# Output products of six heads as seven block products instead of eight, with block sums on GpSimd

## The chip, the cores and the metric

The kernel runs on one core of a Trainium2 chip. The metric is the device time of one execution in microseconds; the profile is one further execution, recorded by the hardware profiler. Engines are named as in the profile: PE is TensorE, DVE is VectorE, ACT is ScalarE, POOL is GpSimd, SP is SyncE, whose queue issues nearly all DMAs.

## What is computed

An encoder trunk of two layers, applied to two independent groups of 512 tokens with 1024 features: one layer of differential attention, one of bidirectional retention. Both end alike, and only that end is touched by the change: a head's 256-wide mixer output is normalised per token, multiplied by a gate, and all eight heads go through one output projection that is added to the residual.

```python
def diff_attention(h, w_in, lq1, lk1, lq2, lk2, subln_g, w_out, lambda_init):
    ...
    o = rms_norm(o, subln_g, SUBLN_EPS) * (1.0 - lambda_init)
    o = o.reshape(B, S, D_INNER) * jax.nn.silu(gate)
    return o @ w_out

def bidir_retention(h, w_in, decay_fwd, decay_bwd, subln_g, w_out):
    ...
    o = rms_norm(o_f + o_b, subln_g, SUBLN_EPS)
    o = o.reshape(B, S, D_INNER) * jax.nn.silu(gate)
    return o @ w_out
```

For one head, one half of a group's tokens and all 1024 output features, the projection is a product of a 256x256 block (tokens by head features) with a 256x1024 block of weights.

## The kernel before

Every fp32 operand of a matmul is split into a high part (cast by ACT, `hi_of`, L481) and a low part (the rest, subtracted by DVE, `lo_of`, L484), and a product is three matmuls (`PASSES`): high by high, high by low, low by high. PE runs, in order: the input projections of layer 1 (to about 610 us; already in seven-product form), the attention heads (to about 1015 us), the input projections of layer 2 (to about 1480 us), the retention blocks, one per head and group (to the end).

In the attention stage a loop runs over 64 tiles (head, group, 128 query tokens): scores (L1546), row maximum on DVE (L1554), exponentials on ACT, a factor from DVE's reciprocal (L1573) and POOL (L1574), a combining add on DVE (L1576), transposes (L1587), and per pair of tiles the product with v (L1607). In the retention stage a block has scores, two states and two chunks of outputs (L1864, L1872; on DVE L1879 and L1883). In both, `weigh` then gates the output (`og`, L1191), splits it into `oT`, and squares it; the two halves of the squares are added on DVE (L1196). `norm_cols` or `weighed_both` turn the squares into `rr`, one factor per token, with a reciprocal root on POOL (L1211, L1912).

`owe` then puts four output steps on the list `todo`, for two token tiles and two column halves of 512. `out_step` issues, for each, six matmuls (two blocks of 128 features by three passes, L1279) into a fresh `pj` bank of PSUM, and one scaled add on DVE (L1284) that multiplies by `rr` and adds to the residual in SBUF. `out_weights` loads 256x512 of weights when they are first needed and splits them with one instruction of 1024 columns each on ACT and DVE. `fill` takes steps from `todo` between other work; `settle` empties a head's steps before the next head reuses its `oT`. There are three `pj` banks; in attention every second transpose takes one too.

None of this is issued at once. Each call records an operation with its engine, an assumed duration and its readers and writers (`Plan.op`); `Plan.arrange` then lists them with a planner: PE takes operations in program order, at most 24 places ahead of the first that isn't done, the others by a due time. `Plan.issue` repeats this with random shifts of due times from the table `SHIFTS` (a time, how far back, how large, what share, a seed). The result is a fixed order for each engine.

Of the kernel before, what the change touches and what calls it, by code (L numbers as in the profile page):

```python
# [10 lines left out]
F32 = mybir.dt.float32  # L11
# [25 lines left out]
LAG = 4  # L37

# [11 lines left out]
class Buf:  # L50
# [237 lines left out]
def trunk_kernel(  # L288
# [22 lines left out]
    places = {}  # L311
    cnt = [0]

    def view(pool, tag, i, size, shape, dt=F32):


        n = math.prod(shape[1:])
        if (tag, i) not in places:
            if size <= 32 and pool in (cp, wk):
                k = next(k for k, used in enumerate(gaps) if used + size <= (1024 + PAD - RING if k < WS_BUFS - 1 else 56))  # L320
                places[tag, i] = pads[k][:, gaps[k]:gaps[k] + size]
                gaps[k] += size
            else:
                places[tag, i] = pool.tile([P, size], F32, tag=f"{tag}{i}", name=f"{tag}_{i}", bufs=1)
        t = places[tag, i][0:shape[0], 0:n]
        if dt != F32:
# [74 lines left out]
    def raw_t(shape, bufs=4):  # L401

        n = math.prod(shape[1:])

        def make(i):
            t = view(wk, "raw", i, n, [P, n]) if i < 4 else both_ring(F32)[:, 0:n]
# [9 lines left out]
    def c_t(name="c"):  # L416
        return work("c", [P, S], 4, name=name)

    def e_t(name="e"):
        return work("e", [P, S], E_BUFS, name=name)  # L420

    def m_t(name="m"):
        return work("m", [P, S], 4, name=name)
# [761 lines left out]
    def weigh(y, sg, oT, c, scale=1.0, sq=None):  # L1185
# [3 lines left out]
        og, sq = c_t("og"), sq or m_t("sq")  # L1189
# [6 lines left out]
        dve(256, lambda: nc.vector.tensor_tensor(sq[:, 0:256], sq[:, 0:256], sq[:, 256:512], op=ALU.add), [sq], [sq])  # L1196
# [93 lines left out]
    def owe(w, h, g, t, o, rr, last):  # L1290
        for i in range(2):
            owed[h, g] = owed.get((h, g), 0) + 1
            parts = 2 if w is wo2 and (h, g, t, i) == (NH - 1, NG - 1, NT - 1, 1) else 1
            todo.append(lambda i=i, parts=parts: out_step(w, h, g, t, i, o, rr, last, parts))

# [300 lines left out]
    def av(i):  # L1596
# [17 lines left out]
        st[i].update(o=o, sq=weigh(o, sg[h, g], oT[h, g], t // 2, GUARD))  # L1614

    def weighed(i):
# [72 lines left out]
    for i in range(FIRST, N + 4, 2):  # L1689
# [13 lines left out]
        fetch_next(i)  # L1703
    while todo:
        fill(1)
# [23 lines left out]
    Fs, aTs, sqs = {}, {}, {}  # L1729
# [13 lines left out]
    def decay(h):  # L1743
# [4 lines left out]
        mid = m_t("mid")  # L1748
        mid2 = m_t("mid")
# [104 lines left out]
    def av2(b, c):  # L1854
# [32 lines left out]
        sqs[b, c] = weigh(y, sg[b], oT[h, g], c, sq=st_t([P, S], "sq"))  # L1887
# [8 lines left out]
    def weighed_both(b):  # L1896
# [7 lines left out]
        for c in range(2):  # L1904
# [7 lines left out]
            pool(200, lambda ss=ss, rr=rr: nc.gpsimd.tensor_tensor(rr.t, ss.t, mhalf[:, 0:2], op=ALU.pow), [ss, mhalf], [rr])  # L1912
            for n in range(2):
# [173 lines left out]
```

## Time and profile before

| | |
|---|---|
| median of 3 runs | 1782.05 us (1781.91 to 1782.11) |
| the profiled execution | 1782.33 us, of which the span is 1780.2 us |
| instructions | 28,644 |
| output products (L1279) | 1,542 matmuls |
| scaled adds (L1284) | 257 |

In the page's first part each engine has its busy time, its share of the span and its instructions. Groups are named by line, engine, operation, and output<-inputs; "busy, mean ns | idle before, releaser" stand behind. A timeline row is a start, a duration, and the instruction, with a wait in brackets. Busy times include the tail of an instruction in which the next may already have begun.

### The profile page before, as it was taken

The numbers are of one execution on the slowest core, as the hardware profiler recorded it, in microseconds if no ns is written. First come the engines' busy times: TensorE is split into PE (matmuls) and PEld (weight loads), VectorE is DVE, ScalarE is ACT, GpSimd is POOL, SyncE is SP. The second block draws the span as 40 slices with busy tenths as digits, with TensorE's granted clock in tenths as the row PEclk, the third lists the DMA queues.
The fourth block names the chain that finished last, engine by engine and source line by source line (L and its number), as shares of the span: only waits on it lengthen the run. The fifth ranks groups of instructions, "written<-read, shape, count | busy, mean of one in ns | idle before, by whom it ended". The sixth has DMA issues, their size and how long they took to land.

```text
span 1780.2 us, 28644 instructions
## 1 busy us (share of the span) xinstructions
PE 1769.7 (99%) x10485; PEld 1565.0 (88%) x10485; DVE 1550.6 (87%) x2660; ACT 926.9 (52%) x1947; POOL 118.5 (7%) x256
## 2 busy tenths in 40 slices
PE   9999999999999999999999999999999999999998
PEld 7889988888998888888888888899889988988887
DVE  8979779999979888888888898887998797888887
ACT  8664434544544565455455876444544455444446
POOL 1000000000000011111111100000000001111114
PEclk9999999999999999999999999999999999999999
DMA  6345535555555695455453624464565579665562
GB/s 233 102 153 168 177 118 160 171 160 168 190 175 155 218 332 187 174 189 190 168 190 105 213 77 155 138 200 166 172 206 179 176 222 407 236 232 194 217 221 95
DMA packets 162819, 328.85 MB, mean 185 GB/s; under 512 B 12772, under 2 KB 76920, under 8 KB 162680
## 3 DMA queue, kind: packets, MB, share of 16 engines
q1 hardware_dynamic: 162352, 326.71, 54.6%
q8 instruction: 82, 1.34, 0.3%
q14 instruction: 57, 0.47, 0.1%
q10 hardware_dynamic: 328, 0.34, 0.1%
HBM read 209.55 MB, written 117.44 MB: 184 GB/s over the span
## 4 chain that ended last, share of the span: by engine, by line
PE 98%; ACT 1%; DMA 1%; DVE 0%; issue 0%; POOL 0%; SPq 0%; POOLq 0%; DVEq 0%; ACTq 0%
PE pj L756 21%; PE pj L1279 19%; PE sc L756 11%; PE pj L766 10%; PE o L756 6%; PE o L1607 5%; PE sc L1546 5%; PE sc L766 5%; PE o L905 3%; PE o L991 2%; PE o L1864 1%; PE tp L1843 1%; PE sc L1816 1%; PE sc L1864 1%; PE pj L1587 1%; PE tp L1587 1%
## 5 line engine op out<-in xcount | busy, mean ns | idle before, releaser
L1279 PE MATMUL pj<-ws,arena 128*128 128x512 f32 (+1 forms) x1334 | 344.8, 390 | 0.0
L1279 PEld LDWEIGHTS pj<-ws,arena 128*128 128x128 f32 x1334 | 247.7, 188 | 50.4
L756 PE MATMUL pj<-b,ws 128*128 128x512 f32 x1080 | 263.5, 390 | 0.0
L481 ACT CAST ws<-st 128x512 fp32r<-128x512 f32 x264 | 161.1, 622 | 162.3 <-PE sc L756 37.5
L756 PEld LDWEIGHTS pj<-b,ws 128*128 128x128 f32 x1080 | 200.0, 188 | 40.4 <-issue 0.3
L484 DVE TENSOR_TENSOR ws<-st,ws 128x512 fp32r<-128x512 f32 x264 | 178.3, 687 | 50.8 <-ACT ws L481 38.4
L1284 DVE SCALAR_TENSOR_TENSOR b<-pj,pad,b 128x512 f32<-128x512 f32 (+1 forms) x257 | 189.6, 745 | 29.8 <-PE pj L1279 16.9
L756 PE MATMUL sc<-arena,ws 128*128 128x512 f32 x768 | 186.0, 390 | 0.0
L756 PEld LDWEIGHTS sc<-arena,ws 128*128 128x128 f32 x768 | 142.7, 188 | 28.9
L756 PE MATMUL pj<-arena,ws 128*128 128x512 f32 x636 | 156.0, 390 | 0.0
L756 PEld LDWEIGHTS pj<-arena,ws 128*128 128x128 f32 x636 | 118.8, 188 | 24.6 <-DVE ws L484 0.2
L481 ACT CAST ws<-raw 128x512 fp32r<-128x512 f32 (+2 forms) x140 | 103.2, 741 | 63.4 <-PE o L905 15.5
L484 DVE TENSOR_TENSOR ws<-raw,ws 128x512 fp32r<-128x512 f32 (+2 forms) x135 | 109.2, 813 | 23.4 <-ACT ws L481 21.1
L1564 ACT ACTIVATE b<-sc,pad 128x512 f32<-128x512 f32 x128 | 87.5, 691 | 74.3 <-DVE pad L1554 74.1
L766 PE MATMUL pj<-ws,b 128*128 128x256 f32 x960 | 116.1, 275 | 0.0
L766 PEld LDWEIGHTS pj<-ws,b 128*128 128x128 f32 x960 | 112.5, 188 | 0.3
L756 PE MATMUL o<-arena,ws 128*128 128x512 f32 x456 | 108.3, 390 | 0.4 <-DVE b L544 0.4
L1546 PE MATMUL sc<-arena 128*128 128x512 f32 x384 | 101.8, 398 | 0.7 <-ACT b L1564 0.7
L809 ACT COPY c<-pj 128x512 f32<-128x512 f32 x96 | 56.3, 588 | 87.1 <-PE pj L756 64.2
L756 PEld LDWEIGHTS o<-arena,ws 128*128 128x128 f32 x456 | 85.3, 188 | 18.3 <-DVE b L544 0.6
L481 ACT CAST os<-e 128x512 fp32r<-128x512 f32 x88 | 54.8, 622 | 77.6 <-DVE e L817 29.2
L1607 PEld LDWEIGHTS o<-arena 128*128 128x128 f32 x768 | 93.0, 188 | 2.4
(307 smaller groups left out, 3233.8 us busy)
## 6 DMA issues: line engine op xcount, KB each, us to landing
qk<-os SPq DMA_DIRECT2D x192, 256.0 KB, 3.6
arena<-qk SPq DMA_DIRECT2D x96, 512.0 KB, 7.0
v<-os SPq DMA_DIRECT2D x64, 512.0 KB, 3.6
arena<-v SPq DMA_DIRECT2D x64, 512.0 KB, 4.1
raw<-in_da_w_in_dram SPq DMA_DIRECT2D x51, 512.0 KB, 5.6
raw<-in_ret_w_in_dram SPq DMA_DIRECT2D x38, 512.0 KB, 5.0
os<-g SPq DMA_DIRECT2D x32, 512.0 KB, 7.2
g<-e SPq DMA_DIRECT2D x48, 256.0 KB, 4.2
```

What stands on the lines that cost most here:

```text
L481: act(n, lambda: nc.scalar.copy(dst(), src()), r, w)
L484: dve(n, lambda: nc.vector.tensor_tensor(dst(), src(), hi().bitcast(F32), op=ALU.subtract), r, w)
L756: nc.tensor.matmul(ps.t, a[u][0]()[:, k, :], bt[k][:, v, :], start=(opens and k == 0 and i == 0), stop=(k == 3 and i == 2), skip_group_che ...
L766: nc.tensor.matmul(ps[:, (t % 2) * 256:(t % 2) * 256 + 256], bt[k][:, v, t * P:(t + 1) * P], a[u][0]()[:, k, :], start=(opens and t % 2 == ...
L809: act(S, lambda c=c, ps=ps: nc.scalar.copy(c.t, ps.t), [ps], [c])
L905: nc.tensor.matmul(ps[:, c0:c0 + 256], w[:, lo:lo + P], of(b, j), start=(start and j == 0 and i == 0), stop=(j == 1 and i == 2), skip_grou ...
L991: nc.tensor.matmul(ps[:, t * 256:t * 256 + 256], of(b, j, t), w[:, a, j], start=(start and t == 0 and j == 0 and i == 0), stop=(j == 1 and ...
L1279: nc.tensor.matmul(ps[:, here], o[a][:, e, t * P:(t + 1) * P], u[b][:, e, here], start=(m == 0), stop=(m == 5))
L1284: axpy(n, lambda half=half, here=here, ps=ps: nc.vector.scalar_tensor_tensor(half, ps[:, here], rr[:, t % 2:t % 2 + 1], half, op0=ALU.mult ...
L1546: nc.tensor.matmul(s.t, q[:, a, t * P:(t + 1) * P], k[:, b, :], start=(n == 0), stop=(n == 2))
L1564: act(840, lambda j=j, s=s, m=m: nc.scalar.activation(p[:, j, :], s.t, AF.Exp, bias=m.t, accum_out=sm[:, 2 * j + n:2 * j + n + 1]), [s, m] ...
L1607: nc.tensor.matmul(o[:, e * 256:(e + 1) * 256], v[b][:, j, e * P:(e + 1) * P], aT[a][:, j, :], start=(n == 0), stop=(n % 12 == 11), skip_g ...
```

## The change

In heads 2, 4 and 6 of the attention layer and 1, 3 and 5 of the retention layer, the output product of a head and a token half is split in two by two by two: tokens in two tiles of 128, features in two blocks of 128, columns in two halves of 512. Its eight block products become seven, P1 to P7. They need sums of blocks of the weights (T1 to T4, once per head, in `fast_weights`) and of the gated output (s1 to s4, for each group and token half, in `block_sums`). The sums are computed on POOL, then split by ACT and DVE; the addition of the squares of these heads moves to POOL as well. Three `pj` banks x, y and z collect the products: x takes P1, P6, P7 and P4 one upon the other, z takes P5 and P3, y takes P2. Each product is followed by a scaled add into one of the four output blocks, so there are seven adds where there were four.

```diff
+FAST = (2, 4, 6,), (1, 3, 5,)
...
-    (635.39, 16, 2, 0.05, 454008), (1473.67, 30, 2, 0.2, 912168), (1473.67, 8, 2, 0.2, 596270),
+    (13.25, 30, 1, 1, 761111), (1599.01, 16, 4, 0.2, 176783), (636.31, 30, 0.3, 0.5, 131788),
...
+    def either(on, n, out, a, b, op, r, w):
+        plan.op(on, 0.2+0.0036*n if on == "POOL" else 0.07 + 0.00104 * n, lambda: (
+            nc.gpsimd if on == "POOL" else nc.vector).tensor_tensor(out(), a(), b(), op=op), r, w)
+
+    def block_sums(og, new):
+        x, hi, lo = st_t([P, S], "sums"), *(n(dt=F32R) for n in new)
...
+        for k, (o, a, b, fn, r) in enumerate((
+                (s1, a21, a22, ALU.add, [og]), (s2, s1, a11, ALU.subtract, [og, (x, 0)]),
+                (s3, a11, a21, ALU.subtract, [og]), (s4, a12, s2, ALU.subtract, [og, (x, 1)]))):
+            either('POOL', P, o, a, b, fn, r, [(x, k)])
+        hi_of(S, lambda: hi.t, lambda: x.t, [x], [hi])
+        lo_of(S, lambda: lo.t, lambda: x.t, lambda: hi.t, [x, hi], [lo])
+        return hi, lo
...
-        dve(256, lambda: nc.vector.tensor_tensor(sq[:, 0:256], sq[:, 0:256], sq[:, 256:512], op=ALU.add), [sq], [sq])
+        if sums is not None:
+            sums.append(block_sums(og, new))
+        either("POOL" if sums is not None else "DVE", 256, lambda: sq[:, 0:256], lambda: sq[:, 0:256],
+               lambda: sq[:, 256:512], ALU.add, [sq], [sq])
...
+    def fast_weights(w, h, t12):
+        r = [raw_t([P, 2, S]) for _ in range(2)]
...
+        hi_of(1024, lambda: hi.t, lambda: r[0].t, [r[0]], [hi])
+        lo_of(1024, lambda: lo.t, lambda: r[0].t, lambda: hi.t, [r[0], hi], [lo])
...
+        either('POOL', S, lambda: x[0].t, b12, b11, ALU.subtract, r, [x[0]])
+        parts("t1", t12[0](), lambda: x[0].t, x[0])
+        either('POOL', S, lambda: x[0].t, b22, lambda: x[0].t, ALU.subtract, [r[1], x[0]], [x[0]])
+        parts("t2", t12[1](), lambda: x[0].t, x[0])
+        either('POOL', S, lambda: x[1].t, b22, b12, ALU.subtract, [r[1]], [x[1]])
+        parts("t3", slot(30, [P, 2, S]), lambda: x[1].t, x[1])
+        either('POOL', S, b21, b21, lambda: x[0].t, ALU.subtract, [r[0], x[0]], [r[0]])
+        parts("b22", ws_t([P, 2, S], 0, WS_BUFS), b22, r[1])
+        late[h] = lambda: parts("t4", ws_t([P, 2, S], 0, WS_BUFS), b21, r[0])
+
+    def fast_owe(h, g, c, o, sums, rr):
...
+        of = dict(P1=(a_of(0, 0), "b11"), P2=(a_of(1, 0), "b21"), P3=(s_of(3), "b22"), P4=(a_of(1, 1), "t4"),
+                  P5=(s_of(0), "t1"), P6=(s_of(1), "t2"), P7=(s_of(2), "t3"))
...
+                for i, (p, q) in enumerate(PASSES):
+                    nc.tensor.matmul(ps.t, a[p](), v[q][0](), start=(start and i == 0), stop=(i == 2),
+                                     skip_group_check=True)
+            pe(0.683, fn, keys + [v[0][1], v[1][1]], [ps])
...
+            axpy(S, lambda: nc.vector.scalar_tensor_tensor(
+                half, ps.t, rr[:, t:t + 1], half, op0=ALU.mult, op1=ALU.add), [ps, (x, i), rr], [(x, i)])
+
+        def first():
+            late.pop(h, lambda: None)()
+            mult("P1", "x", True)
+            added("x", 0, 0)
+            mult("P2", "y", True)
+            added("y", 0, 0)
+        def second():
+            mult("P5", "z", True)
+            added("z", 1, 1)
+            mult("P6", "x")
+            added("x", 0, 1)
+        def third():
+            mult("P7", "x")
+            added("x", 1, 1)
+        def fourth():
+            mult("P3", "z")
+            added("z", 0, 1)
+            mult("P4", "x")
+            added("x", 1, 0)
...
+        if h in FAST[0]:
+            fast_owe(h, g, t // 2, oT[h, g], st[i]['sums'][0], rr)
+            return
...
+            if h in FAST[1]:
+                fast_owe(h, g, c, oT[h, g], fast[b, c][0], rr)
+                continue
...
+            if blocks[b][1] == 0 and blocks[b][0] in FAST[1]:
+                fast_weights(wo2, blocks[b][0], [lambda: raw_t([P, 2, S], 4, F32R)] * 2)
```

The split sums and weights stand in work buffers that are retyped for it (`e`, `m`, `c` and `raw` tiles as the matmul's type). `SHIFTS` is another table, of 89 entries instead of 45, so the planner's order changes over the whole kernel. Line numbers shift: in the changed kernel the output steps are L1321 and L1326, the seven products L1395 with their adds L1402, `lo_of` is L505, scores, transposes and v products of attention are L1685, L1726 and L1746, the softmax factor is L1713, and `either` is L1208.

Three places show what the orders make of it. First PE in the attention stage, at the first output products of head 2, before: two column halves of one token tile between the scores (`sc` banks) of later tiles, six matmuls each into one `pj` bank.

```order
L1546 MATMUL sc_252<-arena 128x512 x3
L1546 MATMUL sc_332<-arena 128x512 x3
L1279 MATMUL pj_357<-ws_88,arena 128x512
L1279 MATMUL pj_357<-ws_76,arena 128x512
L1279 MATMUL pj_357<-ws_88,arena 128x512 x2
L1279 MATMUL pj_357<-ws_76,arena 128x512
L1279 MATMUL pj_357<-ws_88,arena 128x512
L1279 MATMUL pj_406<-ws_84,arena 128x512
L1279 MATMUL pj_406<-both_6170,arena 128x512
L1279 MATMUL pj_406<-ws_84,arena 128x512 x2
```

The same place of the changed kernel: P1, P2, P5 and P6 of that head, three matmuls each (`pj_294` is x, `pj_345` is y, `pj_407` is z; the `e` tiles hold the split block sums, `b_6651` and `b_6734` the weights T1 and T2).

```order
L1685 MATMUL sc_330<-arena 128x512 x3
L1395 MATMUL pj_294<-ws_78,arena 128x512
L1395 MATMUL pj_294<-ws_80,arena 128x512
L1395 MATMUL pj_294<-ws_78,arena 128x512
L1395 MATMUL pj_345<-ws_78,arena 128x512
L1395 MATMUL pj_345<-ws_80,arena 128x512
L1395 MATMUL pj_345<-ws_78,arena 128x512
L1395 MATMUL pj_407<-b_6651,e_180_6784 128x512 x2
L1395 MATMUL pj_407<-b_6651,e_181_6790 128x512
L1395 MATMUL pj_294<-b_6734,e_180_6784 128x512 x2
L1395 MATMUL pj_294<-b_6734,e_181_6790 128x512
```

Where PE filled a bank with six matmuls and left it to DVE, it now fills one with three and comes back to x six matmuls later, once DVE has read it.

Second, DVE in the retention stage, before: scaled adds (`b<-pj`) between the outputs' products (L1883), a gating product, and two sums of squares (L1196).

```order
L1284 SCALAR_TENSOR_TENSOR b_236<-pj_294,pad_83,b_236 128x512
L1883 TENSOR_TENSOR e_543<-sc_252,e_543 128x512
L1284 SCALAR_TENSOR_TENSOR b_236<-pj_357,pad_83,b_236 128x512
L484 TENSOR_TENSOR arena<-c_526,arena 128x2x256
L1196 TENSOR_TENSOR st_679<-st_679 128x256
L1196 TENSOR_TENSOR st_718<-st_718 128x256
L1284 SCALAR_TENSOR_TENSOR b_237<-pj_406,pad_83,b_237 128x512
L1284 SCALAR_TENSOR_TENSOR b_237<-pj_294,pad_83,b_237 128x512
L1191 TENSOR_TENSOR c_590<-e_543,os_369 128x512
L1284 SCALAR_TENSOR_TENSOR b_238<-pj_357,pad_83,b_238 128x512
```

A stretch of the changed kernel in head 1's output steps (`c_216` is the low part of a block sum, `L2024` the far product of an output):

```order
L1402 SCALAR_TENSOR_TENSOR b_238<-pj_345,pad_83,b_238 128x512
L2024 TENSOR_TENSOR e_193_9666<-o_333,b_13970 128x512
L1402 SCALAR_TENSOR_TENSOR b_239<-pj_294,pad_83,b_239 128x512
L505 TENSOR_TENSOR c_216_14406<-st_532,m_215_14372 128x512
L1402 SCALAR_TENSOR_TENSOR b_238<-pj_345,pad_83,b_238 128x512
L1402 SCALAR_TENSOR_TENSOR b_238<-pj_407,pad_83,b_238 128x512
L505 TENSOR_TENSOR b_14378<-tp_303,b_14378 128x256
L1402 SCALAR_TENSOR_TENSOR b_238<-pj_294,pad_83,b_238 128x512
L1402 SCALAR_TENSOR_TENSOR b_239<-pj_345,pad_83,b_239 128x512
L2024 TENSOR_TENSOR e_194_9703<-sc_330,b_13970 128x512
L2028 TENSOR_TENSOR e_193_9666<-o_306,e_193_9666 128x512
L1402 SCALAR_TENSOR_TENSOR b_239<-pj_345,pad_83,b_239 128x512
```

Seven adds to the tiles `b_238` and `b_239` stand where four stood, each for a bank that PE takes again, and the sums of squares are gone from between them.

Third, POOL in the attention stage, before: only the softmax factors (L1574), their squares (L1579) and the norm's two instructions (L1619, L1211), on one or two columns.

```order
L1579 TENSOR_TENSOR pad_81<-pad_81 128x2
L1619 TENSOR_TENSOR pad_83<-pad_83,pad_81 128x2
L1211 TENSOR_TENSOR pad_83<-pad_83,pad_77 128x2
L1574 TENSOR_SCALAR pad_81<-pad_81,pad_77 128x1 x2
L1579 TENSOR_TENSOR pad_81<-pad_81 128x2
```

And in the changed kernel, at the start of a fast head (`m_468` is a tile of squares, `raw` holds weights, `st_498` the block sums of `c_500`):

```order
L1208 TENSOR_TENSOR m_468<-m_468 128x256
L1208 TENSOR_TENSOR st_389<-raw_274,raw_266 128x512
L1713 TENSOR_SCALAR pad_81<-pad_81,pad_79 128x1
L1208 TENSOR_TENSOR st_491<-raw_274 128x512
L1208 TENSOR_TENSOR st_498<-c_500 128x128
L1713 TENSOR_SCALAR pad_81<-pad_81,pad_79 128x1
L1208 TENSOR_TENSOR st_389<-raw_274,st_389 128x512
L1208 TENSOR_TENSOR st_498<-c_500 128x128
L1208 TENSOR_TENSOR st_498<-st_498,c_500 128x128
```

The softmax factors now stand behind weight differences of 512 columns and block sums of 128 in POOL's queue.

More of the change, by code (lines that the diff above doesn't have):

```diff
@@ L310, in trunk_kernel @@
     SIZE = dict(raw=1024, st=512, c=512, e=512, m=512, os=1024)
-    places = {}
+    places, rounded = {}, {}
     cnt = [0]
@@ L324, in view @@
                 places[tag, i] = pool.tile([P, size], F32, tag=f"{tag}{i}", name=f"{tag}_{i}", bufs=1)
+        if dt == F32R and tag in ("e", "c", "m", "raw") or (tag, i) in rounded:
+            if rounded.get((tag, i), F32) != dt:
+                cnt[0] += 1
+                label = f"{tag}_{i}_{cnt[0]}"
+                places[tag, i] = pool.tile([P, size], dt, tag=f"{tag}{i}", name=label, bufs=1)
+            rounded[tag, i] = dt
         t = places[tag, i][0:shape[0], 0:n]
-        if dt != F32:
+        if dt != F32 and (tag, i) not in rounded:
             t = t.bitcast(dt)
@@ new lines, in fast_owe, with a_of, s_of, mult @@
+    def fast_owe(h, g, c, o, sums, rr):
+        banks = {}
+        tiles_ = [xN[g, 2 * c + t] for t in range(2)]
+        def a_of(e, t):
+            lo = (2 * c + t) * P
+            return [(lambda v=v: o[v][:, e, lo:lo + P]) for v in range(2)], [(o[v], c) for v in range(2)]
+        def s_of(k):
+            return [(lambda v=v: sums[v][:, k * P:(k + 1) * P]) for v in range(2)], list(sums)
+        of = dict(P1=(a_of(0, 0), "b11"), P2=(a_of(1, 0), "b21"), P3=(s_of(3), "b22"), P4=(a_of(1, 1), "t4"),
+                  P5=(s_of(0), "t1"), P6=(s_of(1), "t2"), P7=(s_of(2), "t3"))
+        def mult(name, at_, start=False):
+            (a, keys), v = of[name]
+            v = fastw[h][v]
+            if start:
+                banks[at_] = bank("pj")
+            ps = banks[at_]
+            def fn():
+                for i, (p, q) in enumerate(PASSES):
+                    nc.tensor.matmul(ps.t, a[p](), v[q][0](), start=(start and i == 0), stop=(i == 2),
+                                     skip_group_check=True)
+            pe(0.683, fn, keys + [v[0][1], v[1][1]], [ps])
+        def added(at_, t, i):
+            x, ps = tiles_[t], banks[at_]
+            half = x[:, i * S:(i + 1) * S]
+            axpy(S, lambda: nc.vector.scalar_tensor_tensor(
[19 more added lines that the diff above has]
+            added("x", 1, 0)
+        for part in (first, second, third, fourth):
+            owed[h, g] = owed.get((h, g), 0) + 1
+            def one(part=part):
+                owed[h, g] -= 1
+                part()
+            todo.append(one)
@@ L1613, in av @@
             oT[h, g] = new_oT(g)
-        st[i].update(o=o, sq=weigh(o, sg[h, g], oT[h, g], t // 2, GUARD))
+        sums = st[i]['sums'] = [] if h in FAST[0] else None
+        st[i].update(o=o, sq=weigh(o, sg[h, g], oT[h, g], t // 2, GUARD, sums=sums, new=(e_t, e_t)))
     def weighed(i):
@@ L1728, in trunk_kernel @@
     qk, vt, sg, oT = {}, {}, {}, {}
-    Fs, aTs, sqs = {}, {}, {}
+    Fs, aTs, sqs, fast = {}, {}, {}, {}
     kts, Ss = {}, {}
@@ L1886, in av2 @@
             oT[h, g] = new_oT(g)
-        sqs[b, c] = weigh(y, sg[b], oT[h, g], c, sq=st_t([P, S], "sq"))
+        fast[b, c] = [] if h in FAST[1] else None
+        sqs[b, c] = weigh(y, sg[b], oT[h, g], c, sq=st_t([P, S], "sq"), sums=fast[b, c],
+                          new=None if fast[b, c] is None else (m_t, c_t))
     def weighed2(b, c):
```

43 lines of the change are left out of this document (31 added, 12 removed), and 40 rows, old and new, of the table SHIFTS.

## The prediction

> **What bounds the kernel now.** I read the page's table of engines first, then its chain of work.
>
> ```profile
> span 1780.2 us, 28644 instructions
> PE 1769.7 (99%) x10485; PEld 1565.0 (88%) x10485; DVE 1550.6 (87%) x2660; ACT 926.9 (52%) x1947; POOL 118.5 (7%) x256
> PE 98%; ACT 1%; DMA 1%; DVE 0%; issue 0%; POOL 0%; SPq 0%; POOLq 0%; DVEq 0%; ACTq 0%
> ```
>
> TensorE (PE) works for 99% of the span and carries 98% of the chain; VectorE (DVE) stands at 87%. The change touches two stages only, so I asked for windows inside them: the attention heads, then the retention blocks (start:end, length, then busy time of PE, PEld, DVE, ACT, POOL, the granted clock, DMA share, GB/s).
>
> ```profile
> 640.00:980.00 340.00, 340.00 (x1981) 299.54 (x1980) 290.84 (x503) 174.33 (x478) 51.01 (x145) 1.00 0.51 186
> 1560.00:1640.00 80.00, 80.00 (x481) 70.85 (x480) 68.69 (x117) 34.37 (x92) 11.16 (x20) 1.00 0.59 224
> ```
>
> In both PE never pauses and its clock is full, so a matmul taken away here is time won, as long as nobody makes PE wait. DVE has 49 of 340 us free in the first window (14%) and 11 of 80 in the second. ACT is half idle, POOL mostly.
>
> **What the change removes.** For each of six heads, two groups and two token halves, eight block products become seven, each of three 128x512 matmuls: 6 x 2 x 2 x 3 = 72 fewer. PE's order agrees, 10,405 instructions against 10,477. One line of the chain prices them, and it and two lines of the timeline price what else is on PE here:
>
> ```profile
> 149.89 5.50 PE pj L766 x48
> ...
> 1600.09 5.49 PE pj L1279 x24
> ```
>
> ```profile
> 791.76 0.60 PE L1587 MATMUL tp<-ident,b 128*128 128x128 f32 x4
> 792.20 0.60 PE L1587 MATMUL pj<-ident,b 128*128 128x128 f32 x4
> ```
>
> 24 matmuls of 512 columns in 5.49 us are 0.228 us each; those of 256 columns cost 0.114 (5.50/48), a transpose 0.11 (four from 791.76 to 792.20). So **PE loses 72 x 0.228 = 16.4 us**.
>
> **What it adds to DVE.** A busy figure counts the tail of an instruction; what one costs a full engine is the distance from its start to the next start, read where DVE runs without a gap:
>
> ```profile
> 782.18 1.28 DVE L1554 TENSOR_REDUCE pad<-sc 128x1 f32<-128x512 f32 x2
> 783.38 0.41 DVE L1196 TENSOR_TENSOR m<-m 128x256 f32<-128x256 f32 x1
> ...
> 785.03 0.15 DVE L1573 RECIPROCAL pad<-pad 128x1 f32<-128x1 f32 x1
> 785.12 0.75 DVE L1284 SCALAR_TENSOR_TENSOR b<-pj,pad,b 128x512 f32<-128x512 f32 x1
> ...
> 1527.52 0.28 DVE L1752 TENSOR_SCALAR m<-b,pad 128x128 f32<-128x128 f32 x1
> 1527.71 0.69 DVE L1191 TENSOR_TENSOR c<-e,os 128x512 f32<-128x512 f32 x1
> ...
> 1741.50 0.42 DVE L484 TENSOR_TENSOR b<-tp,b 128x256 fp32r<-128x256 f32 x1
> 1741.83 0.41 DVE L1196 TENSOR_TENSOR st<-st 128x256 f32<-128x256 f32 x1
> ...
> 1745.83 0.74 DVE L1284 SCALAR_TENSOR_TENSOR b<-pj,pad,b 128x512 f32<-128x512 f32 x1
> 1746.49 0.68 DVE L484 TENSOR_TENSOR arena<-c,arena 128x512 fp32r<-128x512 f32 x1
> 1747.09 1.22 DVE L484 TENSOR_TENSOR ws<-raw,ws 128x1024 fp32r<-128x1024 f32 x1
> 1748.22 1.40 DVE L1284 SCALAR_TENSOR_TENSOR b<-pj,pad,b 128x512 f32<-128x512 f32 x2
> ```
>
> That gives 0.66 us for a scaled add (1745.83 to 1746.49), 0.60 for two tensors of 512 columns and for a row maximum (two from 782.18 to 783.38), 1.13 for 1024 columns, 0.33 for 256, 0.19 for 128, 0.09 for a reciprocal. For each of the 24 (head, group, half) that take seven products, DVE gets 7 scaled adds for 4 and one more low part of 512 columns, and gives its sum of squares (0.33) to POOL; each of the six heads splits weights in six instructions instead of two. That is 24 x (1.98 + 0.60 - 0.33) + 6 x (1.13 + 5 x 0.60 - 2 x 1.13) = 54 + 11 = 65 us, four times what PE loses. Whether it fits must be counted where it stands.
>
> Attention: I counted the rows of one head's length, from the first row maximum of head 3 to that of head 4, where head 2's seven products run. DVE had 24 scaled adds, 16 row maxima, 16 of 512 columns, 4 of 256, 2 of 1024, 8 reciprocals = 15.8 + 9.6 + 9.6 + 1.3 + 2.3 + 0.7 = 39.3 us. It now has 36, 16, 14, 2, 2 and 8 = 23.8 + 9.6 + 8.4 + 0.7 + 2.3 + 0.7 = 45.5. PE had 144 matmuls of 512, 96 of 256 and 40 transposes = 32.8 + 10.9 + 4.4 = 48.1, and now has 132, 96 and 36 = 45.0. DVE is 0.5 us longer than PE; in the ordinary head behind it DVE has some 4 us to spare. Price per fast head: nothing if queues carry the 0.5 us over, the whole saving of 12 x 0.228 = 2.7 if they carry nothing that varies within the head. I take the 0.5, **1.5 us for the three heads**.
>
> Retention: the fast heads are 1, 3 and 5, and PE's products have been put off to wait for DVE. From the first such stretch of adds (the DVE order shown in the section on the change starts a dozen rows into it) to the last of head 5 there are 280 DVE rows: 106 scaled adds, 126 of 512, 28 of 256, 8 of 1024, 12 of 128 columns = 70.0 + 75.6 + 9.2 + 9.0 + 2.3 = 166.1 us. On PE, between the two products they belong to, stand 417 matmuls of 512, 552 of 256 and 40 transposes = 95.1 + 62.9 + 4.4 = 162.4. **DVE becomes the bound over this stretch, by 3.7 us.** Below this it can't fall in this order; above it stand DVE's own waits.
>
> Those waits I bound by the scaled adds' row, asked for from 1520 to 1700 us alone (idle time ahead of them, and its releasers):
>
> ```profile
> L1284 DVE SCALAR_TENSOR_TENSOR b<-pj,pad,b 128x512 f32<-128x512 f32 x80 | 58.6, 747 | 13.2 <-POOL pad L1912 7.8 <-PE pj L1279 5.4
> ```
>
> The 5.4 us of waiting for PE goes when DVE is late. The 7.8 us for POOL's reciprocal root are hidden today and cost up to 7.8 if they stay. From 1741.50 to 1748.22 DVE ran gapless, so zero is the other end, nearer since every wait can be covered by the backlog of adds. **I take 2 us.**
>
> **What it adds to POOL and ACT.** POOL gets 96 instructions of 128 columns, 24 of 256 and 24 of 512; ACT 48 casts of some 0.6 us, hidden in its half-idle span. No DMA is added: SP's queue has 774 instructions in both. POOL's prices:
>
> ```profile
> L1931 POOL TENSOR_TENSOR e<-b,cos 128x512 f32<-128x512 f32 x7 | 9.4, 1342 | 0.0
> ...
> L1579 POOL TENSOR_TENSOR pad<-pad 128x2 f32<-128x2 f32 x32 | 6.3, 196 | 603.3 <-DVE pad L1573 603.3
> ```
>
> Between 0.20 us for 2 columns and 1.34 for 512 lie 0.48 for 128 and 0.77 for 256, my estimates: 46 + 18 + 32 = 96 us, in stretches of together some 250. POOL has room, but its queue is in order: the softmax factor (L1574) may stand 1.34 us behind a weight difference, the combining add (L1576) waits for it on DVE, and every DVE row behind that, with the transposes on PE. I count that in the 2 us.
>
> The other cost is a collision. This timeline of before shows POOL's root twice, once beside a DVE instruction with both inputs in SBUF:
>
> ```profile
> 1546.38 0.68 DVE L484 TENSOR_TENSOR arena<-c,arena 128x512 fp32r<-128x512 f32 x1
> 1546.40 1.23 POOL L1912 TENSOR_TENSOR pad<-pad,pad 128x2 f32<-128x2 f32 x1
> 1547.61 0.21 POOL L1911 TENSOR_SCALAR pad<-pad 128x2 f32<-128x2 f32 x1
> 1547.66 1.41 DVE L1284 SCALAR_TENSOR_TENSOR b<-pj,pad,b 128x512 f32<-128x512 f32 x2 [0.60 <-POOL pad L1912]
> 1547.90 0.70 POOL L1912 TENSOR_TENSOR pad<-pad,pad 128x2 f32<-128x2 f32 x1
> ```
>
> Beside L484 it took 1.23 us, beside L1284 (one input in PSUM) 0.70: POOL was held for 0.53 us, until DVE was done. Whether POOL holds DVE in turn no row shows; its instructions here move two columns. If it does, the new ones hold for their streaming time (price less 0.20): 96 x 0.28 + 24 x 0.57 + 24 x 1.14 = 68 us. Nearly a third of DVE's time in these stages goes to such instructions by the order, so at most some 0.3 x 68 = 20 us are lost; the least is nothing, and less than nothing is out, since a wait only adds. Since DVE meets a hold part-way through and an ordinary attention head can absorb some, **I take 4 us**.
>
> The Trainium skill, page "SBUF — State Buffer", section "Who interferes with whom", says that a DVE instruction with two SBUF inputs contends with a GpSimd instruction that reads SBUF, and that whichever starts first blocks the other to its end. The 0.53 us agree in one direction; by that rule the term would lie towards 20 us, and against the change.
>
> **Sum:** -16.4 + 1.5 + 3.7 + 2 + 4 = -5.2 us. The profiled execution took 1782.3 (2.1 outside its span), 0.3 above the median of the three runs, so 1777.1 on its scale, **1777 us** as a median.
>
> **Rivals.**
> - *PE keeps its pace.* If the backlog also hides DVE's 3.7 us and the holds are short, little but 16.4 us comes out: 1766 to 1770, say 1768. For it: 49 us of DVE idle in 340. Against: the 166 against 162. Chance 0.17.
> - *GpSimd's holds on DVE's second input.* The place is the saturated DVE in the fast heads; beyond 16.4 - 1.5 - 3.7 - 2 = 9.2 us of holds the kernel is slower than before, at the full 20 us it takes 1793. For it: the 0.53 us. Against: no row shows this direction. Chance 0.18, with about 1788 in the middle. This is the mechanism of the page named above.
> - *POOL's results come late.* The 7.8 us of waits stay, in front of a DVE that has no slack: -16.4 + 1.5 + 3.7 + 7.8 + 4 = +0.6, 1783, no change. Chance 0.12.
> - That the change does not do what it says is out: the 72 matmuls are missing in PE's order.
>
> **Chances and range.** My forecast, 1772.5 to 1781.5, gets 0.53. A measurement of this kernel tells some 0.2% (3.6 us) from no change, so two thirds of it are faster (0.35), the rest the same (0.18). Faster: 0.35 + 0.17 = 0.52; same: 0.18 + 0.12 = 0.30; slower: 0.18. From 1768 to 1788 the range leaves out half of the second rival and the low end of the first, some 0.15.
>
> **What would show it.** PE should have 72 instructions fewer and, for the first time, idle time in the retention windows, some 4 to 8 us in 1520 to 1700, released by DVE's scaled adds; DVE should be above 95% busy there and near 97% while fast attention heads run. The collision is right if DVE instructions with two SBUF inputs last longer than 0.68 us beside a POOL instruction. I am wrong on the bound if PE stays at 100% in the blocks, and on the size if DVE's idle time there exceeds 10 us.

## The result, and the profile after

| | before | after |
|---|---|---|
| median, same chip | 1782.08 us (1781.91 to 1782.11, 4 runs) | 1796.41 us (1793.79 to 1797.77, 4 runs) |
| ratio to before | 1 | 1.0079 (95% interval 1.0064 to 1.0094) |
| span of the profiled execution | 1780.2 us | 1792.0 us |

The change makes the kernel 0.8% slower, and lets its runs scatter by 4 us where those of before on this chip lay within 0.2. The page of the kernel after (span, engines, chain of work):

```profile
span 1792.0 us, 28784 instructions
PE 1767.0 (99%) x10413; PEld 1550.0 (86%) x10413; DVE 1623.8 (91%) x2755; ACT 951.1 (53%) x1996; POOL 239.1 (13%) x400
PE 79%; DVE 14%; DMA 2%; issue 2%; ACT 1%; POOL 1%; ACTq 0%; POOLq 0%; DVEq 0%; SPq 0%
```

The 72 matmuls are gone, yet 14% of the chain now lies on DVE, which had 0%. The two windows that the prediction used:

```profile
640.00:980.00 340.00, 336.80 (x1958) 291.62 (x1958) 326.05 (x546) 187.54 (x499) 109.76 (x216) 1.00 0.52 188
1560.00:1640.00 80.00, 77.84 (x462) 67.23 (x462) 78.72 (x131) 36.82 (x94) 28.34 (x40) 1.00 0.58 210
```

DVE is busy for 78.7 of 80 us in retention, and PE has 3.2 and 2.2 us of idle time. That is too little for what was lost: PE ran 481 matmuls in the second window before, and 462 now, although there are fewer of the long ones among them. A matmul of 512 columns is recorded for 0.39 us but the next starts 0.228 behind it, so PE looks busy through a late start of up to 0.16 us. So I summed, over all PE rows, the time from a start to the next start beyond the usual one for its shape (0.227, 0.114 and 0.109 us for 512, 256 and 128 columns). In the two windows these late starts come to 1.4 and 0.6 us before, and to 8.4 and 5.8 after. In us, by stage (the columns are rounded and their edges are set by hand, so a row can miss its sum by 0.2):

| late starts of PE | to the first scores | attention | 130 us behind it | to retention | retention | sum |
|---|---|---|---|---|---|---|
| before | 9.8 | 2.7 | 0.8 | 1.2 | 2.7 | 17.4 |
| after | 10.4 | 10.5 | 3.3 | 1.0 | 20.1 | 45.4 |

28.0 us more, against the 16.4 of the matmuls, give 11.6 of the 11.8 us by which the span grew. What makes PE late shows in these two stretches of the timeline of after, in attention heads 2 and 4, while the sums for their block products are made:

```profile
719.00 1.31 POOL L1208 TENSOR_TENSOR st<-raw,raw 128x512 f32<-128x512 f32 x1
719.08 1.78 DVE L1715 SCALAR_TENSOR_TENSOR b<-b,pad 128x512 f32<-128x512 f32 x1 [0.48 <-POOL pad L1713]
720.26 1.74 POOL L1208 TENSOR_TENSOR st<-raw 128x512 f32<-128x512 f32 x1
720.78 2.29 DVE L505 TENSOR_TENSOR ws<-raw,ws 128x1024 fp32r<-128x1024 f32 x1
720.91 0.66 PE L1726 MATMUL pj<-ident,b 128*128 128x128 f32 x4
...
828.26 1.84 DVE L1715 SCALAR_TENSOR_TENSOR b<-b,pad 128x512 f32<-128x512 f32 x1
828.28 1.28 POOL L1208 TENSOR_TENSOR st<-raw,st 128x512 f32<-128x512 f32 x1
...
830.16 0.66 PE L1726 MATMUL pj<-ident,b 128*128 128x128 f32 x4 [0.98 <-DVE b L1715]
```

GpSimd starts a weight difference at 719.00, and the combining add (L1715, both inputs in SBUF) that starts 0.08 us later takes 1.78 us, to 0.55 us behind GpSimd's end; it took 0.744 in the mean before. Then it goes round: GpSimd's next difference needs 1.74 us and ends at 722.00, and DVE's low part of 1024 columns 2.29, to 1.07 behind that. At 828.26 an add is held again, for 1.1 us, and PE's transposes wait 0.98 us for it. I call the time by which such a DVE instruction is stretched a hold. Summing every DVE instruction that lasts over 0.1 us longer than the median of its group gives **17.4 us of holds in 37 instructions, each of them beside a GpSimd instruction**; 9.9 us lie in attention, 7.5 in retention. In before there is none. Two of the 37 (L1895, 0.2 us each) read one tensor and a column of factors, so a second whole tensor from SBUF was not needed for a hold.

### The profile page after: what moved, and what is told of

It is laid out like the page before. It is cut to its first block, busy times and chain, and to the rows that moved or that the text cites. A ratio compares the mean times of both kernels' runs of the same rounds, so it can differ in the third digit from the quotient of the medians.

```text
span 1792.0 us, 28784 instructions
## 1 busy us (share of the span) xinstructions
PE 1767.0 (99%) x10413; PEld 1550.0 (86%) x10413; DVE 1623.8 (91%) x2755; ACT 951.1 (53%) x1996; POOL 239.1 (13%) x400
## 4 chain that ended last, share of the span: by engine, by line
PE 79%; DVE 14%; DMA 2%; issue 2%; ACT 1%; POOL 1%; ACTq 0%; POOLq 0%; DVEq 0%; SPq 0%
PE pj L777 19%; PE sc L777 10%; PE pj L787 10%; PE pj L1321 9%; PE sc L787 5%; PE pj L1395 4%; PE o L777 4%; PE o L1746 4%; PE sc L1685 4%; PE o L926 3%; DVE b L1402 2%; PE o L1012 2%; DVE arena L505 2%; DVE ws L505 1%; DVE b L1326 1%
## 5 line engine op out<-in xcount | busy, mean ns | idle before, releaser
L505 DVE TENSOR_TENSOR ws<-st,ws 128x512 fp32r<-128x512 f32 x264 | 177.9, 685 | 48.5 <-ACT ws L502 28.0
L1321 PE MATMUL pj<-ws,arena 128*128 128x512 f32 x854 | 219.2, 391 | 1.1 <-DVE b L1326 1.0
L1321 PEld LDWEIGHTS pj<-ws,arena 128*128 128x128 f32 x854 | 157.9, 188 | 34.5 <-DVE b L1326 2.4
L505 DVE TENSOR_TENSOR ws<-raw,ws 128x512 fp32r<-128x512 f32 (+2 forms) x141 | 114.6, 816 | 23.8 <-ACT ws L502 21.2
L1326 DVE SCALAR_TENSOR_TENSOR b<-pj,pad,b 128x512 f32<-128x512 f32 (+1 forms) x161 | 117.8, 739 | 12.6 <-PE pj L1321 8.1
L1402 DVE SCALAR_TENSOR_TENSOR b<-pj,pad,b 128x512 f32<-128x512 f32 x168 | 120.6, 741 | 0.4 <-PE pj L1395 0.2
L1685 PE MATMUL sc<-arena 128*128 128x512 f32 x384 | 104.2, 400 | 0.8 <-ACT b L1703 0.8
L1746 PEld LDWEIGHTS o<-arena 128*128 128x128 f32 x768 | 93.0, 188 | 2.5
```

The costliest lines, as they stand in the source:

```text
L505: dve(n, lambda: nc.vector.tensor_tensor(dst(), src(), hi().bitcast(F32), op=ALU.subtract), r, w)
L1321: nc.tensor.matmul(ps[:, here], o[a][:, e, t * P:(t + 1) * P], u[b][:, e, here], start=(m == 0), stop=(m == 5))
L1326: axpy(n, lambda half=half, here=here, ps=ps: nc.vector.scalar_tensor_tensor(half, ps[:, here], rr[:, t % 2:t % 2 + 1], half, op0=ALU.mult ...
L1402: axpy(S, lambda: nc.vector.scalar_tensor_tensor(half, ps.t, rr[:, t:t + 1], half, op0=ALU.mult, op1=ALU.add), [ps, (x, i), rr], [(x, i)])
L1685: nc.tensor.matmul(s.t, q[:, a, t * P:(t + 1) * P], k[:, b, :], start=(n == 0), stop=(n == 2))
L1746: nc.tensor.matmul(o[:, e * 256:(e + 1) * 256], v[b][:, j, e * P:(e + 1) * P], aT[a][:, j, :], start=(n == 0), stop=(n % 12 == 11), skip_g ...
```

## Experiments

All but the searched orders start from the changed kernel. The runs used several chips, so each is set against the median of before on its own chip, and "over before" is that difference; the change stands at +14.3 us, and the 72 matmuls alone would give -16.4.

### Which of GpSimd's instructions hold DVE

Three kernels keep the order and shorten what GpSimd reads: e1_narrow_reads all 144 sums, e2_narrow_weights the 24 weight differences, e3_narrow_sums the rest. The narrowed sums have zeros beyond two columns.

```diff
-        nc.gpsimd.tensor_tensor(out(), a(), b(), op=op)
+        nc.gpsimd.tensor_tensor(out()[:, 0:2], a()[:, 0:2], b()[:, 0:2], op=op)
+        nc.gpsimd.memset(out()[:, 2:n], 0.0)
```

> The changed kernel in the same order, but each of the 144 added GpSimd instructions reads only two columns of its inputs and fills the rest of its output with zeros, so it waits for the same things and hardly reads SBUF; the sums, and with them the output, are not the reference's. Theory A, GpSimd's reads of SBUF hold VectorE instructions whose two inputs both lie in SBUF: some 18 us of stretched VectorE instructions go, 1775 to 1780. Theory B, VectorE has too much work in this order, holds or not: 1792 to 1797, as the changed kernel.

Measured: 1783.92 us (1782.69 to 1785.45), +1.6 over before, ratio 1.0008 (0.9998 to 1.0017). So 12.8 of the 14.3 us come back, though not the gain down to 1775 to 1780 that was expected. One hold of 0.1 us is left, and the group of the combining add (L1721 here) is back at its old duration; first the row of after, then that of e1_narrow_reads:

```profile
L1715 DVE SCALAR_TENSOR_TENSOR b<-b,pad 128x512 f32<-128x512 f32 x64 | 51.4, 805 | 2.9 <-POOL pad L1713 2.7
```

```profile
L1721 DVE SCALAR_TENSOR_TENSOR b<-b,pad 128x512 f32<-128x512 f32 x64 | 47.4, 743 | 2.9 <-POOL pad L1719 2.7
```

The zeros are still written, 0.52 us for 510 columns, and hold nobody: it is the reading. PE's transposes that waited 0.98 us at 830.16 follow those before them without a wait here. GpSimd is also busy for 201.1 us instead of 239.1 in this kernel, but DVE's waits for it are unchanged (2.7 us in both rows).

> As above, but only the 24 weight differences of 512 columns read two columns; the block sums and the sums of squares are as in the change, and the output is not the reference's. Theory A: they hold longest, and most of the stretched instructions in the profile stand beside them, so 10 to 14 us come back, 1782 to 1787. Theory B: no change, 1792 to 1797. If the block sums did the damage: above 1790.

> The other part: the 96 block sums of 128 columns and 24 sums of squares of 256 read two columns, the weight differences are as in the change; the output is not the reference's. Theory A: 3 to 7 us come back, 1789 to 1793. Theory B: no change, 1792 to 1797.

Measured: e2_narrow_weights 1785.98 us (1783.97 to 1788.78), +3.6 over before, as expected; e3_narrow_sums 1794.64 (1793.28 to 1796.38), +12.3, where 1789 to 1793 were expected. The 24 wide differences make 10.7 of the 12.8 us, the 120 narrower sums 2.1, although they read more columns in all.

### Does DVE have too much to do?

e4_four_adds leaves out the 72 scaled adds after P5, P6 and P7, 48 us of DVE's work; e5_narrow_and_four does both edits.

```diff
-    axpy(S, lambda: nc.vector.scalar_tensor_tensor(half, ps.t, ...
+    axpy(S, lambda: None if (at_, t, i) in LEFT_OUT else nc.vector.scalar_tensor_tensor(half, ps.t, ...
```

> The changed kernel in the same order with all its GpSimd work, but three of the seven scaled adds of each product (after P5, P6 and P7) are left out, so VectorE does 72 adds less (48 us) and the output is not the reference's. If the holds cost time only because VectorE has no slack in the fast heads: 1766 to 1772. If each hold costs PE its length whatever VectorE's load: 1776 to 1786.

Measured: 1794.36 us (1793.76 to 1796.49), +12.0: only 2.3 us come back, and both expectations are missed. DVE had room: its rows in the window from 640 to 980 take 307.0 us of 340 instead of 326.1. But PE waits as before at the same holds (compare 828.26 and 830.16 above):

```profile
828.85 1.84 DVE L1716 SCALAR_TENSOR_TENSOR b<-b,pad 128x512 f32<-128x512 f32 x1
828.88 1.27 POOL L1208 TENSOR_TENSOR st<-raw,st 128x512 f32<-128x512 f32 x1
...
830.75 0.66 PE L1727 MATMUL pj<-ident,b 128*128 128x128 f32 x4 [0.95 <-DVE b L1716]
```

and the holds have grown from 17.4 to 20.7 us. Idle time elsewhere on DVE doesn't absorb a hold in front of a row that PE needs at once. The run can say no more than that: the products stand behind the making of their sums, and in after all but 1.4 of the 17.4 us of holds lie outside the six stretches (750 to 793, 846 to 891, 941 to 985, 1537 to 1574, 1612 to 1649 and 1688 to 1725 us) from which adds were taken. What room on DVE at the holds themselves would do was not tried.

> The changed kernel's order, with both edits at once: GpSimd's sums read only two columns (the rest of their output is zeros), and the 72 scaled adds after P5, P6 and P7 are left out, so the output is not the reference's. e1_narrow_reads alone left PE some 18 us of late starts over what PE would need, 10.8 of them in retention. Theory 'DVE is full' (the rest of the loss is DVE's work, now 53 us less): most of the 18 us come back, 1766 to 1773 us. Rival 'order' (the rest is waits at fixed places of the new order, round trips between PE and DVE over a bank and the wait ahead of layer 2): only a few us come back, 1778 to 1784.

Measured: 1781.07 us (1780.31 to 1782.04), -0.9 over before. The rival's 1778 to 1784: with neither holds nor a full DVE, the order keeps 15.6 us of late starts more than before has, 10.5 of them in retention.

### Shorter pieces, one layer, no layer

e6_quarters does each weight difference as four instructions of 128 columns, with the same numbers. e7_attention_only and e8_no_block_products take block products out, and the planner makes a new order from the same table.

```diff
+                for k in range(4):
+                    here = slice(k * P, (k + 1) * P)
+                    nc.gpsimd.tensor_tensor(out()[:, here], a()[:, here], b()[:, here], op=op)
```

```diff
-FAST = (2, 4, 6,), (1, 3, 5,)
+FAST = (2, 4, 6,), ()
```

In e8_no_block_products both lists are empty.

> The changed kernel's order, where GpSimd does each weight difference of 512 columns as four instructions of 128 columns: the same numbers are read and written. Theory 'a hold lasts to the end of the GpSimd instruction': no single hold is longer than some 0.6 us, and what DVE has to wait between two pieces is less, so 5 to 8 of the 10.4 us that e2_narrow_weights showed come back, 1788 to 1792. Rival 'holds go by the columns read': nothing comes back, and GpSimd is busier by 24 x 0.8 = 19 us: 1796 to 1800.

Measured: 1788.90 us (1787.15 to 1789.71), +6.9: half of the loss goes although GpSimd reads as much as in the change and is busy longer. The same place as 719.00 above:

```profile
718.88 3.16 POOL L1211 TENSOR_TENSOR st<-raw,raw 128x128 f32<-128x128 f32 x4
718.95 0.93 DVE L1721 SCALAR_TENSOR_TENSOR b<-b,pad 128x512 f32<-128x512 f32 x1 [0.48 <-POOL pad L1719]
719.81 1.48 DVE L505 TENSOR_TENSOR ws<-raw,ws 128x1024 fp32r<-128x1024 f32 x1
```

The add takes 0.93 us instead of 1.78, the low part 1.48 instead of 2.29; all holds together are 8.3 us. A hold lasts to the end of the instruction that holds.

> Block products in attention's three heads alone, the planner makes its own order for this. The trace of the changed kernel has PE's late starts at +7.9 us in attention, +2.5 at the start of layer 2 and +17.1 in retention, against 8.2 us of matmuls less in each layer. Theory 'the loss is made where DVE is full and held, stage by stage': -8.2 + 7.9 + 2.5 = +2.2, 1782 to 1787 us. Rival 'the order made by the new table loses time whatever the heads do': 1788 or more. If the attention stage alone gains: 1775 to 1780.

> The changed kernel's code and table of shifts with no head in block products: the work is that of the kernel before, in the order that the new table gives. Theory 'DVE full and held': nothing is left of the loss, 1780 to 1785 us. Rival 'the new table's order loses time by itself': 1787 to 1795.

Measured: e7_attention_only 1788.41 us, +6.4, ratio 1.0038 (1.0024 to 1.0052); e8_no_block_products 1790.80, +8.8, ratio 1.0047 (1.0031 to 1.0064). Both gave the rivals' numbers. e8_no_block_products does the work of before, so 8.8 us are the table's. The planner's own figure for its end says as much: 1778.6 us, where the table of before gives 1773.0. A table found for one program is bad for another, so these two runs can't price a layer, and tell nothing on how well the table suits the change.

### Orders made for the work

e9_guard_in_act keeps the change's order and adds the retention norm's guard inside ScalarE's row sums, so that one GpSimd instruction per root goes.

```diff
-   ps[:, at_], ps[:, at_], AF.Copy, accum_out=ss[:, t:t + 1])
-   nc.gpsimd.tensor_scalar(ss.t, ss.t, 256 * SUB_EPS, None, op0=ALU.add)
+   ps[:, at_], ps[:, at_], AF.Identity, bias=mhalf[:, 2:3], accum_out=ss[:, t:t + 1])
```

> The changed kernel's order; in the retention blocks the guard of the norm is added by ScalarE inside its row sums, so GpSimd's first instruction of each root (L2058, 26 of them, 0.53 us in the mean and 1.85 at 1666) goes and only the power (L2059) is left between ScalarE and DVE. Theory 'the roots are late': DVE's waits on L2059 (3.6 us in 4 waits, each followed by a late PE in retention) go and so does some of what DVE holds GpSimd there; 2 to 5 us come back, 1791 to 1794 us. Rival 'only holds of DVE and DVE's load count': 1795 to 1797.

Measured: 1795.92 us (1795.17 to 1796.69), +13.7. The rival: late roots are not what is missing.

The next three get tables searched for their own work. The search, a hill climb on the planner's figure, used larger prices for GpSimd; quarters and the guard in ScalarE are kept.

```diff
-    AFTER = dict(PE=0.2, DVE=0.12, ACT=0.13, POOL=0.13, SP=0.0)
+    AFTER = dict(PE=0.22, DVE=0.15, ACT=0.17, POOL=0.45, SP=0.0)
...
-FAST = (2, 4, 6,), (1, 3, 5,)
+FAST = (2, 4, 6,), ()
```

So it stands in e12_attention_new_order; e11_both_new_order has all six heads, e13_none_new_order none.

> All six heads in block products; weight differences in quarters as in e6_quarters, the guard in ScalarE as in e9_guard_in_act, and a new table of shifts, searched with larger prices for GpSimd: 0.45 us instead of 0.13 from the end of an instruction to its reader, 0.80 for a power. Theory 'holds and late roots explain the loss beyond the planner's own figure': the planner's figure for this order is 1761.9 with these prices (it gave 1763.8 for the changed kernel, which ran 28 us longer, and 1773.0 for the kernel before, which ran 7 longer); with 7 as before and some 8 us of holds in quarters, 1775 to 1780 us. Rival 'six heads cost too much on DVE in any order': 1783 or more.

> As e11_both_new_order, but with block products in attention's three heads alone, and its own searched table. The planner's figure is 1767.7; with 7 us as before and 4 of holds, 1776 to 1781 us. Rival 'holds in attention eat the gain': 1783 or more.

> Control for the two runs before: no head in block products (the work of the kernel before), with the guard in ScalarE and a table searched in the same way. The planner's figure is 1774.4. If the search and the prices alone make the gain: 1776 to 1780 us; if the gain is the block products': 1781 to 1785.

Measured: e11_both_new_order 1782.33 us (1781.38 to 1784.13), ratio 1.0001 (0.9992 to 1.0011). That lies between its two expectations. **e12_attention_new_order 1777.07 us (1776.87 to 1777.73), ratio 0.9972 (0.9961 to 0.9983), faster than both kernels**, and as expected. e13_none_new_order 1785.28 us (1783.31 to 1787.26), ratio 1.0018 (1.0008 to 1.0027), 0.3 above its range, so the search and its prices by themselves gain nothing (why this order is 3.1 us behind that of before stays open). Block products in attention pay 8.2 us against this control, as much as their 36 matmuls, and 5.1 against the kernel before; PE's late starts are alike in e12_attention_new_order and the control, 20.0 and 20.1 us in all, so the difference between these two is the matmuls. Block products in retention cost 5.3 us on top. Each kernel got one searched order, and the 3.1 us show how far two orders of the same work can lie apart, so 5.3 is not certain to better than that. The windows of e11_both_new_order, then of e12_attention_new_order, say where:

```profile
640.00:980.00 340.00, 339.48 (x1984) 296.08 (x1983) 324.82 (x554) 189.71 (x510) 122.40 (x256) 1.00 0.52 188
1560.00:1640.00 80.00, 77.11 (x467) 66.96 (x465) 78.42 (x128) 38.67 (x96) 28.78 (x45) 1.00 0.59 216
```

```profile
640.00:980.00 340.00, 339.59 (x1996) 296.84 (x1995) 324.39 (x554) 190.00 (x508) 120.13 (x254) 1.00 0.51 186
1560.00:1640.00 80.00, 80.00 (x493) 71.44 (x493) 67.98 (x114) 34.65 (x87) 8.07 (x10) 1.00 0.56 208
```

In attention PE hardly pauses beside a DVE at 95%; in retention, at 98%, it runs 467 matmuls in 80 us instead of 493.

### What is left: the order or the products?

e14_light_new_order takes the work of e5_narrow_and_four and lets the planner know that the adds are missing, with a searched table. e15_new_order_narrow is e11_both_new_order with the narrow reads.

```diff
+            if (at_, t, i) in LEFT_OUT:
+                return
             axpy(S, lambda: nc.vector.scalar_tensor_tensor(
```

> Six heads in block products, GpSimd's sums on two columns, and the 72 adds after P5, P6 and P7 left out of the plan, so that the output is not the reference's; the order is searched for this lighter work with the prices of e11_both_new_order, and the planner's figure is 1758.1. Theory 'the 15 us left in e5_narrow_and_four are the order of a full DVE': 1763 to 1768 us. Rival 'they belong to the block products, round trips over three banks': 1773 to 1779.

> e11_both_new_order with its order as it stands, and GpSimd's sums on two columns (the output is not the reference's). Its trace shows 9.8 us of holds in 43 DVE instructions. Theory 'most of what is left there is holds': 1773 to 1776 us (7 to 9 back, as the ratio of 12.5 to 17.4 in e1_narrow_reads gives). Rival 'DVE's load in retention': 1779 to 1782.

Measured: e14_light_new_order 1768.11 us (1767.99 to 1769.53), -13.8 over before; e15_new_order_narrow 1778.77 (1778.11 to 1780.01), -3.2. Block products over three banks lose next to nothing when DVE has room and is not held. The second run falls between its two expectations: the quarters' holds cost 3.3 us there, and the larger rest goes only with the 72 adds. The window of e14_light_new_order, then that of e15_new_order_narrow:

```profile
1560.00:1640.00 80.00, 80.00 (x502) 71.72 (x501) 73.59 (x125) 41.23 (x97) 19.08 (x60) 1.00 0.59 218
```

```profile
1560.00:1640.00 80.00, 78.67 (x480) 68.81 (x478) 78.59 (x134) 40.10 (x101) 22.89 (x62) 1.00 0.59 216
```

With DVE at 92% PE runs gapless (502 matmuls), with DVE at 98% it doesn't (480). Late starts in retention are 4.1 us in the first and 12.1 in the second, in attention 2.7 and 4.5. An add that is left out is also one read less of a bank that PE waits for, so the pair alone doesn't tell DVE's work from the round trips over the banks. The trace of e15_new_order_narrow does for retention: from the first add of a block product there to the last, 1526.6 to 1710.9 us, DVE was idle for 2.0 us of 184.3. A wait for round trips would have left it idle; it was its work that PE waited for.

## Why the prediction was wrong

It said -5.2 us; +14.3 were measured. The runs give the 30.7 us between the matmuls' -16.4 and the result in steps, each over before on its chip:

| | over before | step |
|---|---|---|
| the change | +14.3 | |
| no holds, its order (e1_narrow_reads) | +1.6 | holds 12.8 |
| no holds, searched order (e15_new_order_narrow) | -3.2 | order 4.7 |
| and 72 adds fewer, its own searched order (e14_light_new_order) | -13.8 | DVE's load 10.7 |
| 72 matmuls | -16.4 | rest 2.6 |

The steps depend on the sequence: in the change's own order, leaving out the adds gave 2.3 us with the holds and 2.5 without, so 10.7 is the price of the load only where the order can make use of the room. The steps between searched orders are uncertain by some 3 us, the distance of e13_none_new_order from before. The searched orders also have the guard in ScalarE and the planner's larger prices, which e9_guard_in_act and e13_none_new_order show to gain nothing alone.

- **"PE loses 72 x 0.228 = 16.4 us"** was right: e14_light_new_order shows 13.8 of it.
- **Holds, "I take 4 us".** The mechanism was right and the size wrong: 12.8 us, from 17.4 us of holds that come near the 20 which the prediction worked out as the most. The place was another than the second rival's, "the saturated DVE in the fast heads": most holds lie where the sums are made, ahead of the stretches of fast products. The step that failed is the discount from 20 to 4, that DVE "meets a hold part-way through and an ordinary attention head can absorb some". In 22 of the 37 holds DVE started within 0.25 us of the start of a GpSimd instruction (0.08 at 719.08), where the hold is nearly whole, and the held row can be the one that PE needs next, as at 828.26. Attention did absorb some: without holds, in e1_narrow_reads, PE's late starts are 5.2 us fewer there, of 9.9 us of holds, but in retention 6.5 of 7.5. The prediction cites the Trainium skill, page "SBUF — State Buffer", section "Who interferes with whom": whichever starts first blocks the other to its end. That fits this trace in the other direction too: the add of 719.08 ended 0.55 us behind GpSimd's end at 720.31.
- **DVE's load, "1.5 us for the three heads" and "DVE becomes the bound over this stretch, by 3.7 us", with 2 us of waits.** Mis-sized: 7.2 in all against 10.7 for the load, and 18.0 with the order and the rest. Attention comes close: late starts of 4.5 us in e15_new_order_narrow against 2.7 before, where the prediction had 1.5 us. In retention they are 12.1 against 2.7, 9.4 more, where it had 3.7 and 2. The trace of after holds the 280 DVE rows that it counted there, the same numbers of each shape: they run from 1551.07 to 1725.22 us and take 174.2 us, not 166.1; 3.7 us are holds, 2.8 are DVE's waits, and 1.6 lie in the prices. In e1_narrow_reads the same rows take 171.1 us, 3.3 of them waits, and PE is late by 9.3 us over them. So DVE did become the bound there; the rest of retention, ahead of these rows and behind them, was not in the count, and no run prices it alone.
- **The order.** The sum has no term for what the new order loses by itself: it was put at nothing without a reason. A searched order gave back 4.7 us; which waits of the change's order these are stays open.
- **The rivals.** The holds' rival named the right mechanism at 1788, and 1793 at most; it had no room for a load and an order that cost more than its sum. "PE keeps its pace" holds only without holds and with room on DVE. "POOL's results come late" counted on 7.8 us of waits: from 1520 to 1700 us DVE waited 1.8 us for the root in after, and in e9_guard_in_act removing 26 of GpSimd's instructions in front of the roots gave 0.6 us, within the runs' scatter.
- **What was to show it** came out in its amounts, and was too weak a test. DVE's scaled adds released 2.3 us of PE's idle time there, not all of it; ScalarE released as many. PE was idle for 6.1 us between 1520 and 1700 (4 to 8 expected), DVE for 2.8 (below 10), by this window of after:

```profile
1520.00:1700.00 180.00, 173.92 (x1048) 150.60 (x1047) 177.25 (x293) 83.54 (x209) 71.53 (x103) 1.00 0.56 204
```

Busy time of PE hides late starts shorter than a matmul's tail; the sum of start-to-start times doesn't.

## What to carry to other kernels

Trading PE's time for DVE's pays only while DVE keeps room in that stage: at 95% the three attention heads gave their 36 matmuls back in full against the control, at 98% the retention heads lost more than they saved. Sums given to GpSimd are not free for a DVE that reads two inputs from SBUF beside them; cut them short, since here a hold lasted to the end of the GpSimd instruction (four pieces of 128 columns gave back 7.4 of 14.3 us). When an order is tuned for one version of a program, compare versions with orders searched for each, beside a control.

## What else the runs showed

GpSimd is held as well, and for longer than one DVE instruction. At the start of layer 2, in after:

```profile
1018.70 0.68 DVE L713 TENSOR_TENSOR st<-raw,raw 128x512 f32<-128x512 f32 x1
1018.95 3.24 POOL L1457 TENSOR_TENSOR pad<-pad,pad 128x1 f32<-128x1 f32 x1 [3.62 <-ACT pad L1450]
1019.30 1.88 DVE L505 TENSOR_TENSOR arena<-m,arena 128x512 fp32r<-128x512 f32 x3
1021.11 0.68 DVE L713 TENSOR_TENSOR st<-st,both 128x512 f32<-128x512 f32 x1
1022.22 1.15 ACT L486 ACTIVATE b<-b,pad 128x1024 f32<-128x1024 f32 x1 [2.38 <-POOL pad L1457]
```

The root of a final row norm took 3.24 us, until five DVE rows with two SBUF inputs, one upon the next, were through. In before its like stood here:

```profile
1019.28 1.20 POOL L1318 TENSOR_TENSOR pad<-pad 128x1 f32<-128x1 f32 x1 [3.26 <-ACT pad L1311]
```

In after, PE then waited for 2.37 us at 1027.88. No run took this wait away alone.

In e1_narrow_reads the clock falls behind the same wait (row of the timeline, then windows):

```profile
1022.93 7.33 PE L777 MATMUL o<-arena,ws 128*128 128x512 f32 x24 [2.38 <-DVE b L565]
```

```profile
1020.00:1026.00 6.00, 3.62 (x16) 2.83 (x14) 5.90 (x10) 5.05 (x10) 0.00 (x0) 0.85 0.00 0
1026.00:1032.00 6.00, 6.00 (x25) 4.86 (x24) 4.67 (x8) 3.52 (x6) 0.00 (x0) 0.87 0.00 0
```

PE's granted clock is 0.85 and 0.87 of full speed in the mean of these windows, and seven matmuls in a row take 0.427 us to the next start instead of 0.227, and the one ahead of them 0.374: 1.5 us lost. In the profiled execution of after the clock stayed at 1.00 there, at a mean of 0.999; its three other runs had a mean of 0.998 and spans 2.4 to 4.0 us longer. That fits such a fall as part of the scatter, but no trace of those runs shows it.
